# Forgetting attention: the value products of four key blocks issued together, and the PSUM buffers split anew

## The chip, the cores and the metric

The kernel runs on one core of one Trainium2 chip. The metric is the device time of one execution in microseconds (us). Engines are named as in the profile: PE (TensorE matmuls), PEld (its weight loads), DVE (VectorE), ACT (ScalarE), POOL (GpSimd), SP (SyncE, which issues the DMAs).

## The reference, cut to what matters

One layer of a decoder trunk: an RMSNorm, one input projection, three mixers (gMLP, HGRN2, forgetting attention), gates, an output projection with a residual, a final RMSNorm. The change lies in the attention: 4096 tokens, 8 heads of 64 channels, all in float32.

```python
def _fox_mixer(q, k, v, f_logit, b_f):
    ...
    log_f = jax.nn.log_sigmoid(f_logit.astype(jnp.float32) + b_f.astype(jnp.float32))
    c = jnp.cumsum(jnp.transpose(log_f, (0, 2, 1)), axis=-1)
    scale = C_HEAD_DIM ** -0.5
    ...
        s = jnp.einsum('bhqd,bhkd->bhqk', qh[:, :, q0:q1], kh[:, :, :q1]).astype(jnp.float32) * scale
        s = s + c[:, :, q0:q1, None] - c[:, :, None, :q1]
        ...
        p = jax.nn.softmax(s, axis=-1)
        outs.append(jnp.einsum('bhqk,bhkd->bhqd', p.astype(vh.dtype), vh[:, :, :q1]))
    ...
```

The result is multiplied by `silu(c_z)` and goes into the output projection.

## The kernel before, in words

Phase 1 (up to line 1069) makes the projections and the other two mixers and stores queries, keys (each as a high and a low part), values, gates and cumulative sums in DRAM. Phase 3 (from line 1391) is the output projection. Phase 2, from line 1074, is the attention.

Phase 2 works in 32 units: 4 pairs of heads `p` times 8 groups `Q` of 512 queries. A unit goes over its `4 * (Q + 1)` key blocks of 128 keys; that makes 576 steps `(u, kb)` in the loop at line 1330. The last four blocks of a unit are on the diagonal and narrower (`q0_of`). Scores stand transposed, keys on the partitions and queries in the free dimension.

One step does, for each of the two heads, a score tile: two products into a `ps_st` buffer (lines 1353, 1356), the exponential on ACT into a tile `pt` of pool `pp` (line 1360), on the diagonal a mask on POOL (line 1365). Then come row-max products, and the values of the step before (`do_pv`, line 1228): two products into `pv`, one for each head and each half of the partitions (line 1238; in the profile `128*64`, four instructions), and the sums of the weights over the keys, `acc`, head 0 on DVE and head 1 on POOL (line 1247).

The row-max pass is a generator, `rowmax` (line 1128). Each `rm_step` issues one product of 128 queries and 512 keys into one of four `ps_sm` buffers (`rm_product`, line 128) and its maximum on DVE (line 137, on the diagonal line 132). It runs ahead of the steps by `LEAD` = 76 products; a step issues two, a third one while it is behind. `rm_tail` turns a unit's maxima into rows (a transpose on PE, line 1166).

At a unit's end `finish_unit` is a generator that `tick(fin)` moves on, once per step: load the gate; `pl`, the sums over the partitions, two products in a `ps_sm` buffer (line 1206); log and exponential on ACT (lines 1210, 1211), a Newton step on DVE and POOL (lines 1213 to 1216), the product with `pv` on DVE (line 1218), the store.

PE's order is the order of the source (`manual_schedule` for PE alone); on the other engines the tile framework places instructions by its own plan. Eight PSUM buffers of 128x512 float32 are in use: two `st`, four `sm`, two `pv`. The loads of keys and values, `load_next`, have 26 slots (`slots`, ten of them with values, `vslots`) and are given back in the loop when the last unit of a head pair passes a group of keys (lines 1334 to 1339).

Of the kernel before, what the change touches and what calls it, by code (L numbers as in the profile page):

```python
# [10 lines left out]
F32 = mybir.dt.float32  # L11
# [5 lines left out]
ALU = mybir.AluOpType  # L17
# [4 lines left out]
P = 128  # L22
# [11 lines left out]
def tile_trunk(  # L34
# [42 lines left out]
    # units of attention whose row maxima are found before the last projections  # L77
# [13 lines left out]
    def rsqrt_small(pool, ssum, n, scale, tag, y=None):  # L91
        """[P, n] sums -> 1/sqrt(sum * scale + EPS), full float32 accuracy."""
# [30 lines left out]
    def rm_product(ps, qb, kb, hi_, diag, tri, dst):  # L123
        """scores of 128 queries and 512 keys of one head, and their row maxima"""
        h, i = divmod(hi_, 4)
        use = P * (i + 1) if diag else 512
        n = max(use, 256)
        nc.tensor.matmul(  # L128
            ps[:, :n], qb[0:66, h, i * P : (i + 1) * P], kb[0:66, h, :n], start=True, stop=True
        )  # L130
        if diag:
            nc.vector.tensor_tensor_reduce(
                ps[:, :use], ps[:, :use], tri[:, 512 - use :], 1.0, -3.0e38,
                op0=ALU.add, op1=ALU.max, accum_out=dst,
            )
        else:
            nc.vector.tensor_reduce(dst, ps[:, :use], axis=AX.X, op=ALU.max)  # L137

    def rm_rows(p, Q, mp, mm, m2):
        """row maxima over all key groups, less the offset: high and low parts, negated"""  # L140
# [16 lines left out]
    # =====================================================================  # L157
    # Phase 1: RMSNorm, input projection, gMLP, HGRN2, FoX operands
    # =====================================================================
    with ExitStack() as p1:  # L160
# [68 lines left out]
        def xnorm(i0, n):  # L229
            """generator: reciprocal RMS of n token tiles from i0."""  # L230
# [8 lines left out]
        def xprep(T, own_norm=False):  # L239
            """generator: hT[T] = (hi, lo), [P, KC, 256] each."""  # L240
# [43 lines left out]
        def setup_gen():  # L284
            # gMLP
# [23 lines left out]
            # keep source position s (partition) <= target position t  # L309
# [7 lines left out]
            # softmax over the single layer, cumulative sum less its first row  # L317
# [17 lines left out]
            # mixing is linear: LayerNorm's gain goes after it, and its offset  # L335
            # becomes off[t, c] = ln_b[c] * sum_s w[t, s] + b_s[t]
# [6 lines left out]
            # masks of the levels inside a block of 32: [source s, targets in second halves]  # L343
# [7 lines left out]
            for li, h in enumerate(levels[2:]):  # L351
# [4 lines left out]
                # s - 2h*n >= 0  # L356
# [4 lines left out]
                # 2h*n + h - 1 - s >= 0  # L361
# [9 lines left out]
            # head selector columns  # L371
# [5 lines left out]
            # carried state, block-diagonal over the two heads of a tile  # L377
# [4 lines left out]
            # scores: zero for good where the source is in a later block than the target  # L382
# [13 lines left out]
        def hgrn(T):  # L396
            """generator for 256 tokens (two chunks), after its inputs are on chip."""
            z, qf, v = Zb.pop(T), Qf.pop(T), Vb[T]
            lb, oml = setup["lb"], setup["oml"]
            # sigmoid(z) = exp(-L), sigmoid(-z) = exp(-(z + L)), L = ln(1 + exp(-z))  # L400
# [28 lines left out]
            for st in range(len(levels) + 4):  # L429
                if st == 1:  # L430
                    dq = sm.tile([P, 8], F32, tag="dq", name="dq")
                    nc.vector.tensor_copy(dq, pd.rearrange("p c n -> p (c n)"))
                    sc = hg_state["sc"][0]  # r, (chunk, a), t
                    hg_state["sc"].rotate(-1)
                    # blocks of 32 on the diagonal, side by side
                    s32 = wk.tile([P, 8, 32], F32, tag="s32", name="s32", bufs=1)  # (chunk, a, r), t
# [6 lines left out]
                # take over the level scores  # L443
# [24 lines left out]
                # q / k times decay to the middle of each block  # L468
                li = st
                if 0 <= li < 7:  # L470
# [14 lines left out]
                    else:  # L485
                        # both heads' targets side by side, each over zeros in the other's rows
# [12 lines left out]
                if st == 7:  # L499
                    # carry terms  # L500
# [29 lines left out]
                # level products: the two heads of a tile go to different banks  # L530
# [87 lines left out]
            # RMS norm over the value channels  # L618
# [14 lines left out]
        def cgen(B):  # L633
# [12 lines left out]
            # log1p(e) = ln(u) + (e - (u - 1)) / u  # L646
# [43 lines left out]
            # reference offsets of each 512-query group, on all partitions  # L690
# [24 lines left out]
        def silu(ps, dst, scale=1.0):  # L715
            """dst = scale * silu(ps), scale a power of two; dst holds scale * ps meanwhile."""
# [775 lines left out]
```

## Time and profile before

| | |
|---|---|
| median of 3 runs | 3517.5 us (3510.7 to 3524.14) |
| profiled execution | span 3516.6 us from the first to the last instruction; no separate time is listed for it, and the median of the runs lies 0.9 above the span |
| busy shares | PE 97%, PEld 73%, DVE 71%, ACT 45%, POOL 40% |
| mean granted PE clock | 0.982 |
| phase 2, 1674 to 3157 us | PE busy 1467, PEld 715, DVE 1248, ACT 737, POOL 895 us of 1483 |

A row of the timeline gives start and duration in us, engine, source line, operation, tiles (out<-in), shape, and how many equal instructions were merged (x4); in brackets the idle time before it and what ended it. A group of instructions shows busy us, mean ns of one, then the engine's idle time before them and who ended it. PE's durations overlap, because matmuls are pipelined; what a product takes of PE's time is the distance from its start to the next start.

### The profile page before, as it was taken

The numbers are of one execution on the slowest core, as the hardware profiler recorded it, in microseconds if no ns is written. First come the engines' busy times: TensorE is split into PE (matmuls) and PEld (weight loads), VectorE is DVE, ScalarE is ACT, GpSimd is POOL, SyncE is SP. The second block draws the span as 40 slices with busy tenths as digits, with TensorE's granted clock in tenths as the row PEclk, the third lists the DMA queues.
The fourth block names the chain that finished last, engine by engine and source line by source line (L and its number), as shares of the span: only waits on it lengthen the run. The fifth ranks groups of instructions, "written<-read, shape, count | busy, mean of one in ns | idle before, by whom it ended". The sixth has DMA issues, their size and how long they took to land.

```text
span 3516.6 us, 63564 instructions
## 1 busy us (share of the span) xinstructions
PE 3417.2 (97%) x24375; PEld 2569.8 (73%) x24375; DVE 2482.6 (71%) x5111; ACT 1584.4 (45%) x2883; POOL 1422.0 (40%) x1468
## 2 busy tenths in 40 slices
PE   7999999999999999988999999999999999999999
PEld 7999999999999998988444444444444444448887
DVE  6467746685467756782798878888889888965554
ACT  6335544356435543452345445454544554562221
POOL 2134422333134322352465466555665666570000
PEclk9999999999999999999799899999999999999999
DMA  5332333214332223212731141014101321013442
GB/s 178 109 94 64 97 127 116 79 53 159 97 104 68 70 85 111 67 49 78 155 77 34 49 118 43 19 41 120 55 28 28 97 64 37 28 64 135 148 146 96
DMA packets 227603, 297.75 MB, mean 85 GB/s; under 512 B 19602, under 2 KB 172448, under 8 KB 227298
## 3 DMA queue, kind: packets, MB, share of 16 engines
q1 hardware_dynamic: 227298, 293.69, 27.7%
q8 instruction: 191, 3.13, 0.4%
q14 instruction: 114, 0.93, 0.1%
HBM read 208.96 MB, written 84.43 MB: 83 GB/s over the span
## 4 chain that ended last, share of the span: by engine, by line
PE 76%; DVE 13%; ACT 4%; POOL 3%; issue 2%; DMA 2%; SPq 0%; DVEq 0%; POOLq 0%; ACTq 0%
PE acc L885 15%; PE pv L1238 13%; PE acc L906 12%; PE o L1430 10%; PE sm L128 9%; PE st L1353 7%; PE st L1356 6%; DVE wlo L211 2%; DVE acc L1247 1%; DMA x<-in_x_dram 1%; DVE mp L137 1%; PE pl L1206 1%; DVE gt L729 1%; DVE xq L494 1%; PE plb L557 1%
## 5 line engine op out<-in xcount | busy, mean ns | idle before, releaser
L1360 ACT ACTIVATE pt<-st,bias 128x512 f32<-128x512 f32 (+3 forms) x1152 | 692.0, 648 | 711.3 <-PE st L1356 699.3
L1247 POOL TENSOR_TENSOR acc<-acc,pt 128x512 f32<-128x512 f32 (+3 forms) x544 | 700.4, 1288 | 479.9 <-ACT pt L1360 469.4
L137 DVE TENSOR_REDUCE mp<-sm 128x1 f32<-128x512 f32 x896 | 590.1, 682 | 100.1 <-PE sm L128 92.3
L1238 PE MATMUL pv<-pt,v 128*64 128x512 f32 (+3 forms) x2304 | 587.7, 589 | 7.2 <-POOL pt L1365 4.5
L885 PE MATMUL acc<-hhi,whi 128*128 128x256 f32 x2048 | 580.7, 288 | 4.2 <-DVE q L718 2.3
L885 PE MATMUL acc<-hhi,wlo 128*128 128x256 f32 x2048 | 568.1, 282 | 0.0
L885 PE MATMUL acc<-hlo,whi 128*128 128x256 f32 x2048 | 567.3, 281 | 0.0
L906 PE MATMUL acc<-whi,hhi 128*128 128x256 f32 (+1 forms) x1792 | 518.3, 289 | 18.6 <-DVE gu L727 16.0
L1247 DVE TENSOR_TENSOR acc<-acc,pt 128x512 f32<-128x512 f32 (+3 forms) x544 | 506.5, 931 | 40.9 <-ACT pt L1360 30.4
L128 PEld LDWEIGHTS sm<-kb,qb 66*128 66x128 f32 x1152 | 218.1, 192 | 416.6 <-DVE mp L137 177.4
L906 PE MATMUL acc<-wlo,hhi 128*128 128x256 f32 (+1 forms) x1792 | 507.3, 283 | 0.0
L906 PE MATMUL acc<-whi,hlo 128*128 128x256 f32 (+1 forms) x1792 | 506.9, 283 | 0.0
L128 PE MATMUL sm<-kb,qb 66*128 66x512 f32 (+2 forms) x1152 | 494.2, 436 | 5.9 <-DVE mp L137 4.5
L1353 PE MATMUL st<-qa,ka 128*128 128x512 f32 (+2 forms) x1152 | 449.3, 392 | 12.4 <-DMA ka<-d_kl 12.4
L1356 PE MATMUL st<-qc,kb 68*128 68x512 f32 (+2 forms) x1152 | 442.3, 386 | 1.1 <-DMA qc<-d_m 1.1
L885 PEld LDWEIGHTS acc<-hhi,whi 128*128 128x128 f32 x2048 | 385.0, 190 | 7.8 <-DVE q L718 2.7
L885 PEld LDWEIGHTS acc<-hlo,whi 128*128 128x128 f32 x2048 | 384.2, 190 | 0.3 <-DVE hlo L273 0.2
L885 PEld LDWEIGHTS acc<-hhi,wlo 128*128 128x128 f32 x2048 | 384.3, 190 | 0.0
L906 PEld LDWEIGHTS acc<-whi,hhi 128*128 128x128 f32 x1792 | 341.9, 191 | 22.4 <-DVE gu L727 16.6
L906 PEld LDWEIGHTS acc<-wlo,hhi 128*128 128x128 f32 x1792 | 342.3, 191 | 0.1
L906 PEld LDWEIGHTS acc<-whi,hlo 128*128 128x128 f32 x1792 | 341.7, 191 | 0.0
L211 DVE SCALAR_TENSOR_TENSOR wlo<-wraw,gT,whi 128x256 fp32r<-128x256 f32 (+1 forms) x480 | 268.6, 600 | 58.1 <-ACT whi L210 56.8
(262 smaller groups left out, 4911.1 us busy)
## 6 DMA issues: line engine op xcount, KB each, us to landing
wraw<-in_w_in_dram SPq DMA_DIRECT2D x120, 512.0 KB
x<-in_x_dram SPq DMA_DIRECT2D x88, 512.0 KB
qa<-d_qh SPq DMA_DIRECT2D x64, 256.0 KB
out_dram<-x SPq DMA_DIRECT2D x31, 512.0 KB
kb<-d_kh SPq DMA_DIRECT2D x38, 256.0 KB
d_kh<-chi SPq DMA_DIRECT2D x32, 256.0 KB
d_kl<-clo SPq DMA_DIRECT2D x32, 256.0 KB
d_qh<-chi SPq DMA_DIRECT2D x32, 256.0 KB
```

Source lines behind the costliest of these rows:

```text
L128: nc.tensor.matmul(ps[:, :n], qb[0:66, h, i * P : (i + 1) * P], kb[0:66, h, :n], start=True, stop=True)
L137: nc.vector.tensor_reduce(dst, ps[:, :use], axis=AX.X, op=ALU.max)
L211: nc.vector.scalar_tensor_tensor(lo[:, k, :n], raw, g, hi[:, k, :n].bitcast(F32), op0=ALU.mult, op1=ALU.subtract)
L494: nc.vector.tensor_tensor(xq[rows, :, r, :].rearrange("p g (n h) -> p g n h", h=h), sl(e), sl(qf), op=ALU.mult,)
L885: nc.tensor.matmul(ps[:, a, :], ww[:, k, cs], hh[:, k, :], start=n == 0, stop=n == 3 * KC - 1)
L906: nc.tensor.matmul(o, hh[:, k, ts_], ww[:, k, :width], start=n == 0, stop=n == 3 * KC - 1)
L1238: nc.tensor.matmul(pv[64 * h : 64 * h + 64, q0:], vt[:, kb % 4, 64 * h : 64 * h + 64], pts[h][:, q0:], start=kb == 0, stop=kb == nkb - 1,)
L1247: eng.tensor_tensor(a[:, q0:], a[:, q0:], pts[h][:, q0:], op=ALU.add)
L1353: nc.tensor.matmul(st[:, qm:], ka_t[g][:, h, cs], qa_t[u % 2][:, h, qm:], start=True, stop=False)
L1356: nc.tensor.matmul(st[:, qm:], kb_t[g][0:68, h, cs], qc_t[u % 2][:, h, qm:], start=False, stop=True)
L1360: nc.scalar.activation(pt[:, q0:], st[:, q0:], AF.Exp, bias=bias_of[u][:, h, kb : kb + 1])
L1430: nc.tensor.matmul(ps, a[:, k % 4, o : o + P], b[k][:, cs], start=n == 0, stop=n == 3 * KC - 1)
```

## The change

- Values: `do_pv` is called once for four key blocks. A group of eight score tiles is collected, and its 16 products (four blocks, two heads, two instructions each) are issued behind the third score tile of the next group.
- Score tiles are issued one by one (`do_tile`), with row-max steps at fixed places between them.
- Row maxima: `rm_pair` makes two products into one buffer of 2x512 and, off the diagonal, takes both maxima in one DVE instruction. Four pairs in a group of four key blocks are eight products, as before.
- PSUM: three `st` buffers of 128x512, two `sm` buffers of 128x2x512, one `pv` buffer.
- Weight sums: head 1's on POOL right after each step; head 0's on DVE with the group's values. The first block is no longer copied; the second step adds the first two tiles. `pp` has 13 buffers in place of 7.
- Unit end: ACT copies `pv` to SBUF first, `pl` goes into the `pv` buffer, and the last product moves from DVE to POOL; there are three POOL products in place of two.
- The slots of keys and values are given back in `do_pv`.

The rest of the diff removes comments. Its core:

```diff
+    def rm_pair(ps, qb, kb, hi_, diag, tri, mp, cj):
+        for n in range(2):
+            rm_matmul(ps[:, n, :], qb, kb, hi_ + n, diag)
+        if diag:
+            for n in range(2):
+                rm_max(ps[:, n, :], hi_ + n, True, tri, mp[:, hi_ + n, cj : cj + 1])
+        else:
+            rm_max(ps, hi_, False, tri, mp[:, hi_ : hi_ + 2, cj])
...
-        pp = p2.enter_context(tc.tile_pool(name="pp", bufs=7))
+        pp = p2.enter_context(tc.tile_pool(name="pp", bufs=13))
...
-        ps_st = p2.enter_context(tc.tile_pool(name="ps_st", bufs=2, space=PSUM))
-        ps_sm = p2.enter_context(tc.tile_pool(name="ps_sm", bufs=4, space=PSUM))
-        ps_pv = p2.enter_context(tc.tile_pool(name="ps_pv", bufs=2, space=PSUM))
+        ps_st = p2.enter_context(tc.tile_pool(name="ps_st", bufs=3, space=PSUM))
+        ps_sm = p2.enter_context(tc.tile_pool(name="ps_sm", bufs=2, space=PSUM))
+        ps_pv = p2.enter_context(tc.tile_pool(name="ps_pv", bufs=1, space=PSUM))
...
-            for _ in range(3 if u == 0 else 6):
+            for _ in range(2 if u == 0 else 3):
                 yield
...
         def finish_unit(u):
             p, Q = units[u]
-            pv = pv_of.pop(u)
             acc = acc_of.pop(u)
-            zt = fs.tile([P, 512], F32, tag="zt", name="zt", bufs=2)
+            t = fs.tile([P, 512], F32, tag="rt", name="rt", bufs=3)
+            nc.scalar.copy(t, pv_of.pop(u))
+            zt = fs.tile([P, 512], F32, tag="zt", name="zt", bufs=1)
             nc.sync.dma_start(zt, d_z[Q][p * P : p * P + P, :])
             yield
-            pl = ps_sm.tile([P, 512], F32, tag="sm", name="pl")
+            pl = ps_pv.tile([P, 512], F32, tag="pv", name="pl")
...
-            nc.vector.tensor_tensor(t, pl, r, op=ALU.mult)
-            nc.vector.tensor_scalar(t, t, -1.0, 2.0, op0=ALU.mult, op1=ALU.add)
-            nc.gpsimd.tensor_tensor(r, r, t, op=ALU.mult)
-            nc.gpsimd.tensor_tensor(r, r, zt, op=ALU.mult)
+            nc.vector.tensor_tensor(n, pl, r, op=ALU.mult)
+            nc.vector.tensor_scalar(n, n, -1.0, 2.0, op0=ALU.mult, op1=ALU.add)
+            nc.gpsimd.tensor_tensor(t, t, zt, op=ALU.mult)
+            nc.gpsimd.tensor_tensor(r, r, n, op=ALU.mult)
             yield
-            nc.vector.tensor_tensor(t, pv, r, op=ALU.mult)
+            nc.gpsimd.tensor_tensor(t, t, r, op=ALU.mult)
             nc.sync.dma_start(d_yc[p][Q], t)
...
+        def do_acc(u, kb, h, pt):
...
+            eng, a = (nc.vector, nc.gpsimd)[h], acc_of[u][h]
+            if Q == 0 and kb == 0:
+                eng.tensor_copy(a, pt)
+            elif Q and kb == 1:
+                eng.tensor_tensor(a, first_pt[h], pt, op=ALU.add)
+            elif kb:
+                eng.tensor_tensor(a[:, q0:], a[:, q0:], pt[:, q0:], op=ALU.add)
...
+        def do_pv(u, j, group):
...
+            for kb, pts in group:
+                q0, _ = q0_of(u, kb)
+                for h in (1, 0):
+                    nc.tensor.matmul(
+                        pv[64 * h : 64 * h + 64, q0:], vt[:, kb % 4, 64 * h : 64 * h + 64], pts[h][:, q0:],
+                        start=kb == 0, stop=kb == nkb - 1,
+                    )
+            for kb, pts in group:
+                do_acc(u, kb, 0, pts[0])
+            if j == Q:
                 fin.append(finish_unit(u))
+                tick(fin)
+            if Q == NJ - 1:
+                slots[0] += 2
+                vslots[0] += 1
...
             for h in range(2):
...
+                pts.append(do_tile(u, kb, h))
+                n = 2 * (kb % 4) + h
+                if h == 1:
+                    do_acc(u, kb, 1, pts[1])
+                if n in (0, 1, 4, 6):
+                    rm_step()
+                if n in (3, 5, 7) and rm_count[0] < 2 * si + LEAD:
+                    rm_step()
+                if n == 2 and pend is not None:
+                    do_pv(*pend)
+                    pend = None
+                if n in (4, 5, 7):
+                    tick(fin)
+            group.append((kb, pts))
+            if kb % 4 == 3:
+                pend, group = (u, kb // 4, group), []
```

More of the change, by code (lines that the diff above doesn't have):

```diff
@@ L121, in make_tri, with rm_matmul @@
         )
-    def rm_product(ps, qb, kb, hi_, diag, tri, dst):
+    def rm_matmul(ps, qb, kb, hi_, diag):
         h, i = divmod(hi_, 4)
-        use = P * (i + 1) if diag else 512
-        n = max(use, 256)
+        n = max(P * (i + 1) if diag else 512, 256)
         nc.tensor.matmul(
@@ L130, in rm_product, with rm_max @@
         )
+    def rm_max(ps, hi_, diag, tri, dst):
         if diag:
+            use = P * (hi_ % 4 + 1)
             nc.vector.tensor_tensor_reduce(
@@ L136, in rm_product @@
         else:
-            nc.vector.tensor_reduce(dst, ps[:, :use], axis=AX.X, op=ALU.max)
+            nc.vector.tensor_reduce(dst, ps, axis=AX.X, op=ALU.max)
+    def rm_product(ps, qb, kb, hi_, diag, tri, dst):
+        rm_matmul(ps, qb, kb, hi_, diag)
+        rm_max(ps, hi_, diag, tri, dst)
+    def rm_pair(ps, qb, kb, hi_, diag, tri, mp, cj):
[6 more added lines that the diff above has]
+            rm_max(ps, hi_, False, tri, mp[:, hi_ : hi_ + 2, cj])
     def rm_rows(p, Q, mp, mm, m2):
@@ L1137, in rowmax @@
                 for cj in range(Q + 1):
-                    for hi_ in range(8):
-                        ps = ps_sm.tile([P, 512], F32, tag="sm", name="sm")
-                        rm_product(
-                            ps, qb, kb_t[p * NJ + cj], hi_, cj == Q, tri, mp[:, hi_, cj : cj + 1]
-                        )
+                    for hi_ in range(0, 8, 2):
+                        ps = ps_sm.tile([P, 2, 512], F32, tag="sm", name="sm")
+                        rm_pair(ps, qb, kb_t[p * NJ + cj], hi_, cj == Q, tri, mp, cj)
                         yield
@@ L1226, in tile_trunk @@
         fin = []
[L1228 removed]
+        first_pt = {}
+        def do_acc(u, kb, h, pt):
+            p, Q = units[u]
+            q0, _ = q0_of(u, kb)
+            if kb == 0:
+                if u not in acc_of:
+                    acc_of[u] = [ac.tile([P, 512], F32, tag=f"acc{i}", name=f"acc{i}") for i in range(2)]
+                first_pt[h] = pt
+            eng, a = (nc.vector, nc.gpsimd)[h], acc_of[u][h]
[6 more added lines that the diff above has]
+        def do_pv(u, j, group):
             p, Q = units[u]
             nkb = 4 * (Q + 1)
[L1231 to L1232 removed]
+            if j == 0:
                 pv_of[u] = ps_pv.tile([P, 512], F32, tag="pv", name="pv")
[L1234 removed]
             pv = pv_of[u]
[L1236 to L1248 removed]
+            vt = v_t[p * NJ + j]
+            for kb, pts in group:
+                q0, _ = q0_of(u, kb)
+                for h in (1, 0):
[6 more added lines that the diff above has]
+            if j == Q:
                 fin.append(finish_unit(u))
+                tick(fin)
+            if Q == NJ - 1:
+                slots[0] += 2
+                vslots[0] += 1
         wo_hi, wo_lo = [], []
@@ L1304, in rm_step @@
                 next(rm)
-                rm_count[0] += 1
+                rm_count[0] += 2
             except StopIteration:
@@ L1328, in tile_trunk, with do_tile @@
             rm_step()
-        pend = None
+        def do_tile(u, kb, h):
+            p, Q = units[u]
+            g = p * NJ + kb // 4
+            cs = slice((kb % 4) * P, (kb % 4) * P + P)
+            q0, diag = q0_of(u, kb)
+            qm = min(q0, 256)
+            st = ps_st.tile([P, 512], F32, tag="st", name="st")
+            nc.tensor.matmul(
+                st[:, qm:], ka_t[g][:, h, cs], qa_t[u % 2][:, h, qm:], start=True, stop=False
+            )
+            nc.tensor.matmul(
+                st[:, qm:], kb_t[g][0:68, h, cs], qc_t[u % 2][:, h, qm:], start=False, stop=True
+            )
+            pt = pp.tile([P, 512], F32, tag="p", name="pt")
+            nc.scalar.activation(
+                pt[:, q0:], st[:, q0:], AF.Exp, bias=bias_of[u][:, h, kb : kb + 1]
+            )
+            if diag:
+                nc.gpsimd.affine_select(
+                    pt[:, q0 : q0 + P], pt[:, q0 : q0 + P], pattern=[[1, P]], compare_op=ALU.is_ge,
+                    fill=0.0, base=0, channel_multiplier=-1,
+                )
+            return pt
+        pend, group = None, []
         for si, (u, kb) in enumerate(steps):
@@ L1332, in tile_trunk @@
             nkb = 4 * (Q + 1)
-            g = p * NJ + kb // 4
-            if Q == NJ - 1 and kb % 4 == 0 and kb > 0:
-                slots[0] += 2
-                vslots[0] += 1
-            if Q == 0 and kb == 0 and p > 0:
-                slots[0] += 2
-                vslots[0] += 1
-            while g not in ka_t:
+            while p * NJ + kb // 4 not in ka_t:
                 load_next()
```

47 lines of the change are left out of this document (1 added, 46 removed).

## The prediction

> **What bounds the kernel now.** I read the page first, then busy time by stretches, then single steps of the attention stage in the timeline. The page says that PE works 97% of the span, and its chain is mostly PE's.
>
> ```profile
> span 3516.6 us, 63564 instructions
> ...
> PE 3417.2 (97%) x24375; PEld 2569.8 (73%) x24375; DVE 2482.6 (71%) x5111; ACT 1584.4 (45%) x2883; POOL 1422.0 (40%) x1468
> ...
> L1360 ACT ACTIVATE pt<-st,bias 128x512 f32<-128x512 f32 (+3 forms) x1152 | 692.0, 648 | 711.3 <-PE st L1356 699.3
> ...
> PE acc L885 15%; PE pv L1238 13%; PE acc L906 12%; PE o L1430 10%; PE sm L128 9%; PE st L1353 7%; PE st L1356 6%; DVE wlo L211 2%; DVE acc L1247 1%; DMA x<-in_x_dram 1%; DVE mp L137 1%; PE pl L1206 1%; DVE gt L729 1%; DVE xq L494 1%; PE plb L557 1%
> ```
>
> The 1152 exponentials are two heads of 576 key blocks, so 576 steps of the loop. The answer by stretches gives the attention stage, from its first score product to its last value product (columns: stretch, its length, busy us of PE, PEld, DVE, ACT, POOL, then clock, DMA share, GB/s).
>
> ```profile
> 1674.00:3157.00 1483.00, 1467.24 (x5867) 715.47 (x5868) 1248.30 (x2159) 737.33 (x1226) 894.76 (x924) 0.98 0.23 62
> ```
>
> PE is busy all the time, but busy is not streaming. One full step, PE alone:
>
> ```profile
> 2641.71 0.40 PE L1356 MATMUL st<-qc,kb 68*128 68x512 f32 x1
> 2641.94 0.39 PE L128 MATMUL sm<-kb,qb 66*128 66x512 f32 x1
> 2642.26 1.08 PE L1238 MATMUL pv<-pt,v 128*64 128x512 f32 x4
> 2643.27 0.50 PE L128 MATMUL sm<-kb,qb 66*128 66x512 f32 x1
> 2643.61 0.40 PE L1353 MATMUL st<-qa,ka 128*128 128x512 f32 x1
> 2643.84 0.40 PE L1356 MATMUL st<-qc,kb 68*128 68x512 f32 x1
> ...
> 2644.86 0.65 PE L1238 MATMUL pv<-pt,v 128*64 128x512 f32 x2
> ```
>
> From start to start, a 128*128 product of 512 columns takes 0.23 (2641.71 to 2641.94, 2643.61 to 2643.84). Before the values it takes 0.32, after them 0.34, and the values themselves (128*64 form) 1.01. The step is 2.60 (2642.26 to 2644.86). At one place the values are followed by the row sums `pl`, which have the same 128*64 form:
>
> ```profile
> 3089.21 1.08 PE L1238 MATMUL pv<-pt,v 128*64 128x512 f32 x4
> 3090.12 1.03 PE L1206 MATMUL pl<-acc,ones_v 128*64 128x512 f32 x4
> 3091.08 0.50 PE L1353 MATMUL st<-qa,ka 128*128 128x512 f32 x1
> 3091.42 0.40 PE L1356 MATMUL st<-qc,kb 68*128 68x512 f32 x1
> ```
>
> There the values take 0.91 (entry, no exit) and the row sums 0.96 (exit, no entry). So with neither they take 0.91 + 0.96 - 1.01 = 0.86. Each change of form costs, and no other engine is behind it: at the end of the stage, with no row maxima left for DVE, the numbers are the same (1.01, then 0.34).
>
> ```profile
> 3074.19 1.08 PE L1238 MATMUL pv<-pt,v 128*64 128x512 f32 x4
> 3075.20 0.50 PE L1353 MATMUL st<-qa,ka 128*128 128x512 f32 x1
> 3075.54 0.40 PE L1356 MATMUL st<-qc,kb 68*128 68x512 f32 x1
> ...
> 3076.34 1.08 PE L1238 MATMUL pv<-pt,v 128*64 128x512 f32 x4
> ```
>
> **The change part by part.** *Values of four key blocks together.* 144 groups replace 576 steps. Of four entries, three go: 3 x (0.32 - 0.23) = 0.27. Of four exits, three go: 3 x (0.34 - 0.23) = 0.33. The values themselves: 0.91 + 2 x 0.86 + 0.96 = 3.59 in place of 4 x 1.01 = 4.04, so 0.45. Together 1.05 us a group, 10.40 to 9.35, and 144 x 1.05 = 151 us. Diagonal blocks are narrower, but I take the cost of a change of form to be the same for them. This is all on the path, since PE's queue is in order and full.
>
> *What has to hide behind the 9.35 us.* I lay out one group from its first score tile: three score tiles (0.47 each) and two row-max pairs until 2.3, the values until 6.0, five tiles and two pairs until 9.35.
>
> DVE has four pair maxima and four sums `acc` of head 0. Its rows:
>
> ```profile
> 2640.83 1.48 DVE L1247 TENSOR_TENSOR acc<-acc,pt 128x512 f32<-128x512 f32 x1
> 2642.23 1.28 DVE L137 TENSOR_REDUCE mp<-sm 128x1 f32<-128x512 f32 x2
> 2643.08 1.27 POOL L1247 TENSOR_TENSOR acc<-acc,pt 128x512 f32<-128x512 f32 x1 [1.33 <-ACT pt L1360]
> 2643.43 1.48 DVE L1247 TENSOR_TENSOR acc<-acc,pt 128x512 f32<-128x512 f32 x1
> ```
>
> ```profile
> L137 DVE TENSOR_REDUCE mp<-sm 128x1 f32<-128x512 f32 x872 | 574.5, 682 | 73.8 <-PE sm L128 66.0
> L1247 DVE TENSOR_TENSOR acc<-acc,pt 128x512 f32<-128x512 f32 x448 | 457.0, 1020 | 33.7 <-ACT pt L1360 30.4 <-POOL pt L1365 1.8
> L132 DVE CUSTOM_DVE_ANT_0 sm<-sm,tri 128x512 f32<-128x512 f32 x58 | 40.1, 691 | 4.0 <-PE sm L128 3.7
> ...
> L132 DVE CUSTOM_DVE_ANT_0 sm<-sm,tri 128x128 f32<-128x128 f32 x58 | 17.6, 303 | 4.3 <-PE sm L128 3.9
> ```
>
> Two maxima take 1.28, that is 0.60 each from start to start. A pair in one instruction is not in this trace. Above it is bounded by 1.20 (two of them), below by streaming alone: (691 - 303) / 384 = 1.01 ns an element, 1.03 for 1024. I take 0.60 + 512 x 1.01 ns = 1.12, because the trace's own slope gives it. A sum takes 0.68 when POOL is quiet (2660.03 below) and 1.48 when it starts while POOL's sum runs: DVE's ends 0.56 after POOL's (2644.91 against 2644.35), so it seems to wait for it. Four sums are thus 2.7 to 5.9. I take 2.7: they are queued behind the second pair, from about 3.4, in PE's values, when the exponentials of tiles 0 to 2 are done and POOL, which now sums head 1 as each block comes, has run out. DVE then has 4 x 1.12 + 2.7 = 7.2 of 9.35, and at the upper end 4.8 + 5.9 = 10.7, which would be the bound.
>
> ACT: eight exponentials at 0.65 are 5.2 of 9.35. Three score buffers let it run on under the values. POOL: four sums at 1.27 are 5.1. The copy of a unit's first block goes on both engines for 28 of the 32 units; all that is off the path.
>
> *Two pair buffers for four single ones.* A pair's product waits for the maximum two pairs back. In the layout the tightest is the second pair of a group (PE at 1.4), whose buffer comes free at about 0.9, so nothing waits. At a unit's end something is late. The values' bank is now one: ACT copies it out, `pl` is put into it, and the next unit's values queue behind the last reader of `pl`, 4.2 us after `pl` ended (three tiles and a pair of its own group, three tiles and two pairs of the next, 0.47 each). The chain in between, in today's rows:
>
> ```profile
> 2658.05 0.60 ACT L1210 ACTIVATE rc<-pl 128x512 f32<-128x512 f32 x1 [1.89 <-PE pl L1206]
> 2658.71 1.27 ACT L1360 ACTIVATE pt<-st,bias 128x512 f32<-128x512 f32 x2
> 2659.86 0.63 ACT L1211 ACTIVATE rc<-rc 128x512 f32<-128x512 f32 x1
> 2660.03 0.68 DVE L1247 TENSOR_TENSOR acc<-acc,pt 128x512 f32<-128x512 f32 x1
> ...
> 2661.47 0.68 DVE L1213 TENSOR_TENSOR rt<-pl,rc 128x512 f32<-128x512 f32 x1
> 2662.07 0.68 DVE L137 TENSOR_REDUCE mp<-sm 128x1 f32<-128x512 f32 x1
> ```
>
> Log, exponential and product are 0.60 + 0.63 + 0.68 = 1.9, and with two or three exponentials between them 3.2 to 3.9: just inside the 4.2. But if DVE stands at that product while the next pair waits behind it, PE gets to the pair after that about 1.5 too early. Here DVE took other work first (the maximum at 2662.07 stands between L1213 and the step that follows it in the source), so I take 0.4 of the 0 to 1.5, for 32 units: 13 us. The transposes of the row maxima share the two pair slots: 29 at 0.3 (0 to 1.0), 9 us. Without row maxima, in the last 9 or so groups, eight exponentials fall into 3.7 us of tiles, and the three buffers run out: 0.6 a group, 6 us. The last group's values now come after the loop: 2 us. SP's queue: the gate's load is issued some steps earlier relative to the unit's end and waits at most for POOL's product of the unit before; key slots come free one or two steps later, with ten of the 26 to spare. Both 0; if that cover failed, a load is a few us for PE, once per head pair.
>
> Phase 1 and the output stage run the same instructions; the output's sums have two slots in place of four, and for each of them 24 products of 0.23, 5.5 us, stand against one DVE sum: 0.
>
> *The sum*, against the profiled span of 3516.6: -151 + 13 + 9 + 6 + 2 = -121, so 3396; the median of the runs is 0.9 above that span: 3397.
>
> **The clock at a unit's end.** PE's clock was halved after a pause in this stage, and not after a shorter one:
>
> ```profile
> 1972.91 1.24 PE L128 MATMUL sm<-kb,qb 66*128 66x512 f32 x4
> 1975.62 0.38 PE L1166 MATMUL mt<-ident,m 128*16 128x128 f32 x1 [1.46 <-DVE mp L132]
> ...
> 2085.06 0.39 PE L128 MATMUL sm<-kb,qb 66*128 66x512 f32 x1
> 2086.33 1.08 PE L1238 MATMUL pv<-pt,v 128*64 128x512 f32 x4 [0.88 <-DVE rt L1218]
> ```
>
> ```profile
> 1976.00:1996.00 20.00, 20.00 (x54) 10.35 (x56) 11.12 (x28) 5.59 (x10) 5.99 (x12) 0.50 0.23 54
> ```
>
> 1.46 idle was followed by 20 us at 0.50, a loss of 10; after 0.88 idle the values had their 1.08, as in a full step. [...]
>
> **The rivals.** *Unit ends halve the clock (slower).* If DVE does stand at the product of `pl`, PE idles 1.5 once per unit, beside the 1.46 above, and each such pause costs 1.5 + 10: 32 x 11.5 = 368, less 151, plus the 17 of the other terms: 3751. It turns slower once more than (151 - 17) / 11.5 = 12 of the 32 units do it. For it: today's four slots become two pairs. Against: today the unit ends pass at less than 1 us idle, and DVE's order moves.
>
> *Unit ends wait, and the clock stays.* The same pauses at their own price alone: 3397 + 32 x 1.5 - 13 = 3432. For it: the 0.88 above. Against: the 1.46.
>
> *DVE becomes the bound.* If the four sums collide with POOL as today's mean of 1.02 has it, DVE needs 4.5 + 4.1 = 8.6, still under 9.35; it takes 1.3 a sum and more to bind. At 10.0 a group the time is 3517 - 0.4 x 144 = 3459; if every sum collides, 10.7 and 3560. For it: today most sums collide. Against: in bursts under the values POOL has little to do.
>
> *The change of form is not what costs.* If each key block's first products pay their entry anew (new weights each time), only the 0.60 around them is saved: 3517 - 86 + 30 = 3461. Against: `pl` above had new weights too.
>
> *Nothing comes of it.* PE waits for DVE at every group end and the period stays 10.4: 3517.
>
> **How the numbers follow.** Forecast 3397: 0.69, own range 3360 to 3430. Waits at unit ends with the clock left: 0.05. DVE the bound: 0.08, three quarters of it faster. Form not the cost: 0.06. Nothing: 0.04. Clock halved at unit ends: 0.08. The range 3355 to 3465 holds the forecast, the second rival and most of the two near 3460: 0.69 + 0.05 + 0.10 = 0.84. Below, all the small terms at 0 would give 3366. Faster by over 0.5% (17.6 us, about what can be told from no change here): 0.69 + 0.05 + 0.06 + 0.06 = 0.86; within it the 0.04 and part of DVE's case, 0.05; slower 0.09.
>
> **What would show it.** In the changed kernel 16 value products stand in a row and take about 3.6 us from the first to the next 128*128 product, with one 0.32 before and one 0.34 after; full groups repeat every 9.3 to 9.4; the stage lasts about 1360. The pair maximum lies at 1.1 to 1.2, DVE's sums at 0.7 each under the values. Wrong would be: sums of 1.3 and more in the bursts, PE idle over 1 us once per unit with the clock at 0.50 behind it, or inner value products that still take 1.0 a block.

## The result, and the profile after

The changed kernel takes 3483.6 us (median of four runs, 3480.4 to 3486.9) against 3514.1 for the kernel before (3507.3 to 3524.1): a ratio of 0.9916, interval 0.989 to 0.9942. It is faster by 0.8%, where the prediction said 3397 and a range of 3355 to 3465. The direction held; some 87 us of the gain are missing. The page of the changed kernel (its profiled execution took 3480.4 us):

```profile
span 3478.6 us, 62964 instructions
PE 3324.5 (96%) x24375; PEld 2627.7 (76%) x24375; DVE 2385.7 (69%) x4615; ACT 1607.1 (46%) x2915; POOL 1458.1 (42%) x1472
PE acc L902 16%; PE pv L1274 13%; PE acc L923 12%; PE o L1475 10%; PE sm L127 6%; PE st L1374 6%; PE st L1377 5%; DVE mp L140 4%; DVE acc L1261 3%; DVE wlo L228 2%; DMA x<-in_x_dram 1%; PE pl L1223 1%; DVE gt L746 1%; DVE xq L511 1%; PE xtp L284 1%
L1261 POOL TENSOR_TENSOR acc<-acc,pt 128x512 f32<-128x512 f32 (+2 forms) x516 | 672.4, 1303 | 329.8 <-ACT pt L1381 302.0
L127 PE MATMUL sm<-kb,qb 66*128 66x512 f32 (+2 forms) x1152 | 367.0, 400 | 61.1 <-DVE mp L140 36.4
```

DVE has less work than before (2385.7 for 2482.6 us), and yet its maxima and sums hold 7% of the chain, where they held 2%: PE now waits for them. The waits of PE in the attention stage between 1680 and 3000 (total, times, longest), before the change:

```profile
PE sm L128 <- DVE mp L137: 4.5, 7, 0.7
PE sm L128 <- DVE mp L132: 0.9, 1, 0.9
```

and after it:

```profile
PE sm L127 <- DVE mp L140: 36.4, 36, 2.2
PE sm L127 <- DVE mp L135: 17.3, 27, 3.0
PE mt L1181 <- DVE mp L140: 1.9, 6, 0.6
```

So PE's waits for a row-max buffer rose from 5.4 to 53.7 us. The mean granted clock also fell, from 0.982 to 0.973: over the two spans the clock took 63 us before (0.018 x 3516.6) and 94 after (0.027 x 3478.6). These 48 and 31 us are most of what is missing. Over the whole attention stage, from its first score product to its last value product, the trace shows 1483 us before: PE pauses for 16 of them and loses 28 at half clock (half of the time at 0.50), which leaves 1439. After the change it shows 1445, with 70 and 59, which leaves 1316. PE's own work thus fell by some 123 us, and pauses and clock gave most of it back. One of the places, in the timeline of the changed kernel:

```profile
2341.76 3.65 PE L1274 MATMUL pv<-pt,v 128*64 128x512 f32 x16
...
2344.07 1.47 DVE L1261 TENSOR_TENSOR acc<-acc,pt 128x512 f32<-128x512 f32 x1
2344.95 1.73 POOL L1235 TENSOR_TENSOR rt<-rt,rc 128x512 f32<-128x512 f32 x1
2345.34 0.50 PE L1374 MATMUL st<-qa,ka 128*128 128x512 f32 x1
...
2345.64 1.59 DVE L1261 TENSOR_TENSOR acc<-acc,pt 128x512 f32<-128x512 f32 x1
2345.69 0.39 PE L1377 MATMUL st<-qc,kb 68*128 68x512 f32 x1
...
2347.01 4.48 POOL L1261 TENSOR_TENSOR acc<-acc,pt 128x512 f32<-128x512 f32 x3 [0.33 <-ACT pt L1381]
2347.15 1.25 DVE L163 TENSOR_TENSOR mm<-mm,cref 128x8 f32<-128x8 f32 x1
2348.33 0.68 DVE L1261 TENSOR_TENSOR acc<-acc,pt 128x512 f32<-128x512 f32 x1
2348.93 1.24 DVE L169 TENSOR_SCALAR m<-mm 128x8 fp32r<-128x8 f32 x1
...
2350.28 1.22 DVE L140 TENSOR_REDUCE mp<-sm 128x2 f32<-128x1024 f32 x1
2351.56 1.17 PE L127 MATMUL sm<-kb,qb 66*128 66x512 f32 x2 [2.21 <-DVE mp L140]
2353.38 0.41 PE L1181 MATMUL mt<-ident,m 128*16 128x128 f32 x1
2354.42 1.22 PE L127 MATMUL sm<-kb,qb 66*128 66x512 f32 x2 [0.62 <-DVE mp L140]
```

The values are as forecast: 16 products in 3.58 (2341.76 to 2345.34), entry 0.32, exit 0.35 (3.59, 0.32, 0.34 said). Behind them the plan goes wrong. DVE's sums stand among the maxima and start while POOL is busy, so they take 1.47 and 1.59; an addition over 128x8 elements, 0.16 where it is undisturbed (row L163 below), takes 1.25, and another small one 1.24. The pair maximum starts at 2350.28, and PE stands until 2351.56. Then the transpose takes one of the two pair buffers, and the next pair waits again. The stretches around it (length, busy us of the engines, clock, DMA share, GB/s) show what the pause costs beyond itself:

```profile
2351.60:2358.50 6.90, 6.28 (x15) 3.09 (x17) 6.06 (x8) 1.37 (x2) 1.78 (x1) 0.51 0.42 92
2358.50:2365.00 6.50, 6.50 (x29) 3.85 (x26) 2.28 (x3) 2.88 (x5) 2.21 (x2) 1.00 0.13 40
```

After 2.21 idle PE ran 6.9 us at 0.51, another 3.4 lost. In this trace half clock also came without one long pause: at 2232.17, 2590.57 and 2952.38 two waits of 0.48 and 0.38 (0.49 and 0.37 at the third), less than the 0.88 that the prediction saw go by, were followed by 3.4 us at half clock (0.50).

### The profile page after: what moved, and what is told of

It is laid out like the page before. It is cut to its first block, busy times and chain, and to the rows that moved or that the text cites. A ratio compares the mean times of both kernels' runs of the same rounds, so it can differ in the third digit from the quotient of the medians.

```text
span 3478.6 us, 62964 instructions
## 1 busy us (share of the span) xinstructions
PE 3324.5 (96%) x24375; PEld 2627.7 (76%) x24375; DVE 2385.7 (69%) x4615; ACT 1607.1 (46%) x2915; POOL 1458.1 (42%) x1472
## 4 chain that ended last, share of the span: by engine, by line
PE 71%; DVE 19%; ACT 4%; issue 3%; DMA 2%; POOL 2%; SPq 0%; DVEq 0%; ACTq 0%; POOLq 0%
PE acc L902 16%; PE pv L1274 13%; PE acc L923 12%; PE o L1475 10%; PE sm L127 6%; PE st L1374 6%; PE st L1377 5%; DVE mp L140 4%; DVE acc L1261 3%; DVE wlo L228 2%; DMA x<-in_x_dram 1%; PE pl L1223 1%; DVE gt L746 1%; DVE xq L511 1%; PE xtp L284 1%
## 5 line engine op out<-in xcount | busy, mean ns | idle before, releaser
L1381 ACT ACTIVATE pt<-st,bias 128x512 f32<-128x512 f32 (+3 forms) x1152 | 698.7, 651 | 630.2 <-PE st L1377 582.3
L1261 POOL TENSOR_TENSOR acc<-acc,pt 128x512 f32<-128x512 f32 (+2 forms) x516 | 672.4, 1303 | 329.8 <-ACT pt L1381 302.0
L140 DVE TENSOR_REDUCE mp<-sm 128x2 f32<-128x1024 f32 (+1 forms) x460 | 534.8, 1192 | 223.5 <-PE sm L127 222.7
L1274 PE MATMUL pv<-pt,v 128*64 128x512 f32 (+3 forms) x2304 | 510.1, 587 | 0.0
L1261 DVE TENSOR_TENSOR acc<-acc,pt 128x512 f32<-128x512 f32 (+2 forms) x516 | 458.8, 889 | 43.1 <-POOL pt L1386 17.1
L1374 PE MATMUL st<-qa,ka 128*128 128x512 f32 (+2 forms) x1152 | 468.4, 409 | 19.6 <-DMA v<-d_v 13.2
L127 PE MATMUL sm<-kb,qb 66*128 66x512 f32 (+2 forms) x1152 | 367.0, 400 | 61.1 <-DVE mp L140 36.4
L1274 PEld LDWEIGHTS pv<-pt,v 128*64 128x64 f32 x2304 | 159.0, 143 | 297.6 <-issue 279.7
L1374 PEld LDWEIGHTS st<-qa,ka 128*128 128x128 f32 x1152 | 221.1, 192 | 191.4 <-issue 133.1
```

What stands on the lines that cost most here:

```text
L127: nc.tensor.matmul(ps[:, :n], qb[0:66, h, i * P : (i + 1) * P], kb[0:66, h, :n], start=True, stop=True)
L140: nc.vector.tensor_reduce(dst, ps, axis=AX.X, op=ALU.max)
L1261: eng.tensor_tensor(a[:, q0:], a[:, q0:], pt[:, q0:], op=ALU.add)
L1274: nc.tensor.matmul(pv[64 * h : 64 * h + 64, q0:], vt[:, kb % 4, 64 * h : 64 * h + 64], pts[h][:, q0:], start=kb == 0, stop=kb == nkb - 1,)
L1374: nc.tensor.matmul(st[:, qm:], ka_t[g][:, h, cs], qa_t[u % 2][:, h, qm:], start=True, stop=False)
L1381: nc.scalar.activation(pt[:, q0:], st[:, q0:], AF.Exp, bias=bias_of[u][:, h, kb : kb + 1])
```

## The experiments

Each was timed against the kernel before on the same chip, which took 3508 to 3515 us there. The bands in the expectations count the changed kernel as 3484 us. Waits and groups are those between 1680 and 3000 us where nothing else is said.

**Is it DVE's order?** VectorE in program order through the attention stage:

```diff
+        order = tc.manual_schedule(engines={mybir.EngineType.DVE})
+        order.__enter__()
         pend, group = None, []
...
         drain(fin)
+        order.__exit__(None, None, None)
```

> VectorE keeps the program's order in the attention stage: two pair maxima, the four sums of head 0 behind the values, then the other pairs; in the changed kernel the scheduler had put sums, row tails and finishing steps between the maxima. Theory O (the order is what makes the pair slots late, as the prediction had it laid out in program order): the 2.3 us waits for a pair slot and the waits of the transposes go, PE's waits of the stage fall from about 131 us to below 60, the stage from 1444.9 to about 1360 to 1390, and the time to 3400 to 3430 us. Rival C (VectorE is late because its sums and small operations stand still beside GpSimd's sums, in whatever order): the waits stay above 100 us and the time within 3465 to 3500 us. Rival D (VectorE has too much work in a group for two pair slots): slower waits at every group, 3480 us or more.

Measured: 3489.1 us, ratio 0.9924 (0.99 to 0.9949); no change. DVE's groups in this run (busy us, mean ns, idle before):

```profile
L1261 DVE TENSOR_TENSOR acc<-acc,pt 128x512 f32<-128x512 f32 x372 | 309.0, 831 | 26.9 <-DVE acc L1261 0.5
L1259 DVE TENSOR_TENSOR acc<-pt 128x512 f32<-128x512 f32 x27 | 35.6, 1320 | 0.0
L1230 DVE TENSOR_TENSOR rn<-pl,rc 128x512 f32<-128x512 f32 x30 | 20.7, 691 | 43.6 <-ACT rc L1228 43.4
```

The sums became quicker (831 for 952 ns; 103 of 372 still overlap an instruction of POOL, 264 of 375 in the changed kernel), but DVE now stood 43.4 us in front of the Newton step, waiting for ScalarE, with the maxima queued behind it. Theory O falls as stated: the order alone gives nothing.

**Is it the transposes' buffer?**

```diff
-            pt = ps_sm.tile([16, P], F32, tag="sm", name="mt")
+            pt = ps_st.tile([16, P], F32, tag="st", name="mt")
```

> The transposed row maxima take a score-tile buffer (three) in place of one of the two pair buffers. Theory S (the 28 waits of 1.1 us at the transposes are the price of one pair buffer in two): these 31 us go, with the half-clock stretches behind them, and the time falls by 30 to 45 us to about 3440 to 3455. Rival O or C (VectorE is late at these places, and whoever is next waits): the waits move to a score tile or to the next pair, and the time stays within 3470 to 3495.

Measured: 3449.0 us, ratio 0.9807 (0.9779 to 0.9835): 35 us better than the changed kernel, theory S. PE's waits between 1680 and 3000 are now

```profile
PE sm L127 <- DVE mp L135: 18.6, 28, 3.0
PE sm L127 <- DVE mp L140: 17.7, 17, 2.3
```

so the waits for the pair maxima (L140) halved, those for the diagonal (L135) stayed.

**Is it GpSimd's sums?**

```diff
-                nc.tensor.matmul(pl[64 * h : 64 * h + 64, :], ones_v, acc[h], start=True, stop=True)
+                nc.tensor.matmul(pl[64 * h : 64 * h + 64, :], ones_v, acc[0], start=True, stop=True)
...
-                if h == 1:
-                    do_acc(u, kb, 1, pts[1])
```

> Left out: head 1's sums on GpSimd (both halves of the divisor come from head 0's sums). Theory C (collisions with GpSimd make VectorE late): the sums of head 0 fall from a mean of 889 ns to about 650, the 128x8 operations from up to 1.25 us to about 0.1, the waits of PE in the stage from 131 us to below 50 and the time to 3385 to 3420. Theory O (the order alone): the sums are shorter but still stand ahead of the maxima; waits of 80 to 110 us are left and the time is 3440 to 3470.

Measured: 3400.4 us, ratio 0.9677 (0.9656 to 0.9698): 83 us better, theory C. DVE's full sums and PE's waits for row maxima:

```profile
L1261 DVE TENSOR_TENSOR acc<-acc,pt 128x512 f32<-128x512 f32 x405 | 309.6, 764 | 26.4 <-ACT pt L1381 13.7 <-DVE acc L1261 0.5 <-POOL pt L1386 0.3
PE sm L127 <- DVE mp L140: 22.9, 28, 2.0
PE sm L127 <- DVE mp L135: 3.6, 8, 1.1
```

The sums fell from 952 to 764 ns, not to the 650 expected: 58 of the 405 still meet other work of POOL, mostly the products of a unit's end, and take 1234; the other 347 take 686. The waits halved, and the mean clock rose from 0.973 to 0.985. The same edit in the kernel before is the control:

> The kernel before without head 1's sums on GpSimd (left out; both halves of the divisor come from head 0's sums), as a control. If the collisions of VectorE's and GpSimd's sums cost time only where two pair buffers have replaced four single ones, the kernel before gains little: its waits for a product slot are about 11 us in the stage, so 3490 to 3512 us. If they cost the kernel before as much as the changed one (about 80 us), 3420 to 3450 us, and the collisions explain nothing of the missing gain.

Measured: 3490.1 us, ratio 0.9922 (0.9895 to 0.9948), some 25 us. The kernel before pays for the collisions too, but less than a third as much.

**Is it DVE's amount of work?**

```diff
-            nc.vector.tensor_reduce(dst, ps, axis=AX.X, op=ALU.max)
+            nc.vector.tensor_reduce(dst, ps[..., :64], axis=AX.X, op=ALU.max)
```

> Left out: the pair maxima off the diagonal read only 64 of 512 columns of each product. If VectorE's time to free a pair buffer is what stops PE (theories O and C both), its waits in the stage fall below 30 us, the half clock goes with them, the stage comes to about 1310 to 1340 and the time to 3345 to 3380: that is the floor that PE's own work sets in this form. Rival E (PE waits for ScalarE's exponentials, score buffers or value loads once the pair buffers are free): 3400 us or more, with the waits at the score tiles.

Measured: 3440.6 us, ratio 0.9788 (0.9763 to 0.9813), 43 us better; the expected floor was missed by 60. DVE's groups between 1680 and 3000, first of the changed kernel:

```profile
L140 DVE TENSOR_REDUCE mp<-sm 128x2 f32<-128x1024 f32 x427 | 508.7, 1220 | 193.0 <-PE sm L127 192.4
L1261 DVE TENSOR_TENSOR acc<-acc,pt 128x512 f32<-128x512 f32 x375 | 357.0, 952 | 12.9 <-POOL pt L1386 1.5 <-DVE acc L1261 0.5
L163 DVE TENSOR_TENSOR mm<-mp,cref 128x8 f32<-128x8 f32 x3 | 0.5, 157 | 0.0
```

then of this run:

```profile
L1261 DVE TENSOR_TENSOR acc<-acc,pt 128x512 f32<-128x512 f32 x391 | 517.5, 1323 | 41.7 <-POOL pt L1386 23.0 <-ACT pt L1381 7.9
L140 DVE TENSOR_REDUCE mp<-sm 128x2 f32<-128x128 f32 x432 | 121.2, 283 | 261.4 <-PE sm L127 261.4
```

387 us of maxima were taken away, and the sums took 160 of them back (391 of them for 375): a DVE that is free sooner starts its next sum beside POOL's work. In this run 374 of the 391 sums overlap it, in the changed kernel 264 of 375. PE kept 37.7 us of waits for row maxima (22.0 and 15.7). So neither rival: it was not ScalarE, and it is not work alone but when it starts.

**Are buffer and collisions two costs?** Both single edits together:

> Two single edits together: the transposed row maxima in a score-tile buffer, and no sums on GpSimd (left out as in the run without them). If the price of the pair buffer and the price of the collisions are separate costs, the gains of 35 and 83 us add up to 3360 to 3375 us; if both are the same lateness of VectorE, the second gives nothing on top of the first: 3390 to 3405 us.

Measured: 3370.9 us, ratio 0.9593 (0.9576 to 0.9609): they add up nearly, 113 us of 35 + 83. PE's waits for row maxima are nearly gone and clean groups follow each other every 9.32 (2205.81 to 2215.13 in the timeline):

```profile
PE sm L127 <- DVE mp L135: 3.6, 8, 1.1
PE sm L127 <- DVE mp L140: 1.5, 5, 0.5
```

```profile
2205.81 3.65 PE L1274 MATMUL pv<-pt,v 128*64 128x512 f32 x16
2215.13 3.65 PE L1274 MATMUL pv<-pt,v 128*64 128x512 f32 x16
```

**What does a batch cost?** The run with both single edits, with a group's values in two batches, behind tiles three and seven (`do_pv` then takes which half; that part of the edit is not shown):

```diff
-                if n == 2 and pend is not None:
-                    do_pv(*pend)
-                    pend = None
-                if n in (4, 5, 7):
+                if n in (2, 6) and pend is not None:
+                    do_pv(*pend, n // 4)
+                    if n == 6:
+                        pend = None
+                if n in (0, 1, 7):
```

> The run with the score-tile buffer for the transposes and without GpSimd's sums (3371 us, PE almost without waits), but the values of a group in two batches of two blocks, behind tiles three and seven, in place of one batch of four (a unit's end moves with the second batch). By the prediction's term a batch costs 1.05 / 3 = 0.35 us for going over to the values' form and back, so 144 batches more cost about 50 us: 3410 to 3435 us. Rival N (the change of form isn't what cost, and the stage became shorter by the dropped waits): 3365 to 3385 us.

Measured: 3432.7 us, ratio 0.9769 (0.9743 to 0.9795), 62 us more. But the unit's end, moved along, makes PE wait:

```profile
PE pv L1275 <- DVE rn L1230: 22.4, 27, 1.4
```

Without these 22.4 it is 39 us for 144 batches, 0.27 each, where the term had 0.35: the change of form does cost, and rival N falls. A batch of full width can be read in this run's timeline directly:

```profile
2207.83 0.39 PE L1380 MATMUL st<-qc,kb 68*128 68x512 f32 x1
2208.15 1.94 PE L1275 MATMUL pv<-pt,v 128*64 128x512 f32 x8
2210.02 0.50 PE L1377 MATMUL st<-qa,ka 128*128 128x512 f32 x1
2210.36 0.40 PE L1380 MATMUL st<-qc,kb 68*128 68x512 f32 x1
```

Eight products take 1.87, with 0.32 before and 0.34 after. The second batch thus costs 2 x 1.87 - 3.58 = 0.16 inside and 0.09 + 0.11 at its ends, 0.36 in all, the price of the prediction. That the run as a whole shows 0.27 fits the narrower batches on the diagonal, which were not summed.

**Is it the pairs?** Four single buffers and two maxima in the same banks:

```diff
-        ps_sm = p2.enter_context(tc.tile_pool(name="ps_sm", bufs=2, space=PSUM))
+        ps_sm = p2.enter_context(tc.tile_pool(name="ps_sm", bufs=4, space=PSUM))
...
-                        ps = ps_sm.tile([P, 2, 512], F32, tag="sm", name="sm")
-                        rm_pair(ps, qb, kb_t[p * NJ + cj], hi_, cj == Q, tri, mp, cj)
+                        for m in (hi_, hi_ + 1):
+                            ps = ps_sm.tile([P, 512], F32, tag="sm", name="sm")
+                            rm_product(ps, qb, kb_t[p * NJ + cj], m, cj == Q, tri, mp[:, m, cj : cj + 1])
```

> The changed kernel with four single buffers for the row maxima and a maximum of 512 columns for each product, as before the change, in the same four banks; all else as changed. If two pair buffers are what makes the changed kernel sensitive to a late VectorE, the waits for a product slot fall although VectorE has more work (two maxima of about 0.69 us for one of 1.22): 3440 to 3470 us. If VectorE's lateness is what counts, however the banks are cut, the extra 0.15 us a pair (580 pairs) make it no better: 3480 to 3520 us.

Measured: 3417.7 us, ratio 0.9724 (0.9697 to 0.9752), 66 us better, and below the lower band. DVE has more to do (1127 for 1062 us between 1680 and 3000) and PE waits less:

```profile
PE sm L127 <- DVE mp L140: 10.1, 17, 1.5
PE sm L127 <- DVE mp L135: 2.5, 4, 0.8
```

A pair buffer comes free only when both products are read, a single one after its own. With GpSimd's sums left out as well:

> The changed kernel with four single buffers for the row maxima (3418 us alone) and without GpSimd's sums (left out; 3400 us alone with pair buffers). If the two are separate costs they add up (66 + 83 us): about 3335 to 3350 us. If they are one cost, a late VectorE that only a pair buffer passes on to PE, little is left for the second edit: 3370 to 3400 us, about where the pairs without GpSimd's sums and with a buffer apart for the transposes stand (3371).

Measured: 3360.9 us, ratio 0.9574 (0.955 to 0.9597), between the two bands. The medians side by side:

| us | with GpSimd's sums | without |
|---|---|---|
| kernel before | 3514 | 3490 |
| changed kernel, two pair buffers | 3484 | 3400 |
| pairs, transposes in a score-tile buffer | 3449 | 3371 |
| four single buffers | 3418 | 3361 |

Single buffers gain 66 us with the sums and 39 without; moving the transposes alone gives 29 there, so most of the 39 may be theirs. Separate costs would have given 66 + 83 = 149 us; 123 came. So they overlap by 26 (31 by the ratios, since the runs are from different chips), and the rest is separate.

The pairs alone in the kernel before:

> The kernel before with only the row maxima changed: two pair buffers in the same four banks and one maximum for a pair, values still two products for each key block. If pair buffers pass VectorE's lateness on whatever the values do, the time rises by 20 to 70 us to 3535 to 3585, with the unit's end (its divisor takes a pair buffer too) worst. If pair buffers hurt only where VectorE gets four sums at once, behind the batch of values, the time stays at 3495 to 3525 us.

Measured: 3688.4 us, ratio 1.0507 (1.048 to 1.0533). It does not answer the question. A full step still takes 2.60 (2699.88 to 2702.48), and off the diagonal PE hardly waits for a pair (L149); its new waits between 1680 and 3100 are on the diagonal:

```profile
PE sm L128 <- DVE mp L132: 76.7, 108, 3.3
PE sm L146 <- DVE mp L149: 0.3, 1, 0.3
```

That is the edit's own doing. On the diagonal its `rm_pair` issues product, maximum, product, maximum into one buffer, and the second product waits for the first maximum (0.74 at 2186.02, 1.47 at 2190.20); the changed kernel issues both products first. Half clock comes with it: over the stage it takes 110 us for 28 before (granted clock 0.93 from 1674 to 3200, against 0.98). What pair buffers cost where the values are not batched stays open, but for the 0.3 us off the diagonal.

**Versions with the whole computation.** First, transposes in a score-tile buffer, DVE in program order, and the Newton step moved behind a step of its own:

```diff
             nc.scalar.activation(r, r, AF.Exp, scale=-1.0)
+            yield
             nc.vector.tensor_tensor(n, pl, r, op=ALU.mult)
```

> The whole computation; transposed row maxima in a score-tile buffer, VectorE in the program's order, and the two Newton steps of a unit's end one step later than ScalarE's logarithm and exponential. With VectorE's order alone the time did not move: the last groups of a unit became longer by 1.5 us (11.3 for 9.8), where VectorE stood in front of the Newton step until ScalarE was done (50 us in the stage), and the other groups shorter. If that wait ate the gain, the time falls to 3400 to 3425 us; if the order has nothing to give beside the collisions, it stays at the 3440 to 3455 of the buffer alone.

Measured: 3446.9 us, ratio 0.981 (0.9792 to 0.9829), the same as the buffer alone. Then GpSimd in program order too, with its sum of a first block held back behind the second's:

```diff
-                if h == 1:
-                    do_acc(u, kb, 1, pts[1])
+                if n == 3:
+                    do = [(kb - 1, group[0][1][1]), (kb, pts[1])]
+                    for b, t in do if kb == 1 else do[::-1]:
+                        do_acc(u, b, 1, t)
+                elif n in (5, 7):
+                    do_acc(u, kb, 1, pts[1])
```

> As the run before, with GpSimd too in the program's order, and its sum of a group's first block behind the sum of the second, so that no sum of GpSimd falls beside the value products, where VectorE has its own four. If collisions are what is left, VectorE's sums come near 690 ns (from 852 in program order), and the time is 3370 to 3400 us, near the run without GpSimd's sums; if GpSimd's own lateness comes in their place (the mask of the diagonal and the unit's end behind the sums), 3410 us or more.

Measured: 3401.4 us, ratio 0.968 (0.966 to 0.9699): the best whole version, 82 us below the changed kernel. In its timeline DVE's sums lie under the values at 0.76 each, and POOL's four stand beside DVE's maxima:

```profile
2216.44 1.89 PE L1274 MATMUL pv<-pt,v 128*64 128x512 f32 x8
2216.51 2.28 DVE L1261 TENSOR_TENSOR acc<-acc,pt 128x512 f32<-128x512 f32 x3
2219.86 5.36 POOL L1261 TENSOR_TENSOR acc<-acc,pt 128x512 f32<-128x512 f32 x4 [4.14 <-ACT pt L1381]
2219.96 1.23 DVE L140 TENSOR_REDUCE mp<-sm 128x2 f32<-128x1024 f32 x1 [1.17 <-PE sm L127]
2221.36 1.23 DVE L140 TENSOR_REDUCE mp<-sm 128x2 f32<-128x1024 f32 x1 [0.17 <-PE sm L127]
2222.76 2.36 DVE L140 TENSOR_REDUCE mp<-sm 128x2 f32<-128x1024 f32 x2 [0.17 <-PE sm L127]
```

The sums' mean came down to 825 ns, not to 690: elsewhere they still meet POOL. The moved sum without DVE's order:

> The run at 3401 us without the program order on VectorE: GpSimd alone is in program order, with its sum of a group's first block moved behind the second's; transposes in a score-tile buffer, Newton steps one step later. If the collisions fall only where both engines' orders fit, the time goes back to 3430 to 3455 us; if moving GpSimd's sum is enough, it stays at 3395 to 3415.

Measured: 3419.7 us, ratio 0.9731 (0.97 to 0.9763), between the bands: 29 us below the run with the transposes' buffer alone come with GpSimd's order, its moved sum and the later Newton steps, which were not tried apart, and 18 us need DVE's order as well. With single buffers:

> The whole computation: four single buffers, the transposes among them, with VectorE and GpSimd in program order, GpSimd's sum of a first block behind the second's, and the Newton steps one step later. If the costs are separate, the single buffers give some 20 to 35 us beside the 3401 of the same order with pairs: 3365 to 3385 us. If they are one cost: 3390 to 3405. If the two maxima for a pair (0.15 us more on VectorE) are now too much beside the sums in program order: above 3405.

Measured: 3403.8 us, ratio 0.9693 (0.9666 to 0.972): nothing on top. Where DVE is in time, cutting the banks anew gains nothing in sum; the transposes share the four buffers again here, so a small gain and a small cost may cancel. Last, ScalarE in program order:

> The run at 3401 us with ScalarE as well in program order, up to the first split of the output projection's inputs. There two casts of that split stand among the last exponentials and wait for a load, and PE waits 3.7 and 3.1 us for score tiles and then runs at half clock. If these casts are the whole cause, the two waits go and the time falls by 5 to 12 us to about 3390 to 3396; if the casts are then late for the output projection, the gain is given back there: 3398 to 3405.

Measured: 3422.1 us, ratio 0.9739 (0.9713 to 0.9766), worse than both bands. The two long waits at the end went, but PE now waits for ScalarE at unit ends throughout the stage and in the last unit (`PE st L1374 <- ACT pt L1381` 11.9 us at 32 places between 1680 and 3010, for 0.9 at three in the version at 3401). At the two places that were followed, 2145.80 and 2990.51, the logarithm and exponential of a unit's end stand before the exponentials of the score tiles, at the second also a cast of the output weights. The output stage begins with 2.3 us of waiting for a cast of its inputs.

## Why the prediction was wrong

*Values of four blocks, -151: right in kind, somewhat too large.* In full groups the form costs what was read from one place before, and clean groups come every 9.32 (9.35 said). Over the stage, PE's time without pauses and half clock fell by less, from 1439 to 1316 us in the changed kernel and to 1306 in the run with both single edits; the groups on the diagonal, taken at the full price, are the likely difference, not a shown one. With GpSimd's sums out of both kernels the change gives 3490 - 3371 = 119 us with the transposes moved and 129 with single buffers; the forecast's whole sum was 121. That these meet is partly luck: the values gave less, and the 13 us for unit ends and 9 for transposes are not in those runs.

*DVE's sums at 0.68 under the values: this step failed.* It put POOL at rest there and DVE's sums in a burst in program order. Neither was so: DVE's order is the scheduler's, and POOL's sums run through the group. The sums took 952 ns on average, the prediction's own sign of being wrong (1.3 and more in the bursts) came with the 1.47 and 1.59 above, and what is worse, a late sum delays the maximum behind it. The prediction held DVE's total against the period (7.2 of 9.35, "still under 9.35" even with collisions) and missed that two pair buffers give a maximum no room to be late. That is the 83 us of the run without GpSimd's sums, less the 25 of the control: some 58 of the 87 that are missing. The rival "DVE becomes the bound" had the cause and nearly the time (3459), but not the mechanism: DVE still idles 193 us before its pair maxima, and taking three quarters of their time away gave 43 us. Two sizes were off beside this: by its own rows DVE binds from (9.35 - 4.5) / 4 = 1.2 a sum, not 1.3, and the pair maximum took 1.22, over the 1.20 that was to bound it.

*Two pair buffers: wrong.* "Nothing waits" became 53.7 us, four single buffers in the same banks are 66 us faster, and the transposes, put at 0.3 each and 9 us, are worth 35 (29 without GpSimd's sums): 1.0 to 1.2 for each of 29, at their upper end of 1.0 or past it. These 29 and the 58 above are the 87.

*Unit ends: right in that PE does not wait for the product of `pl`*; that wait is not in the changed kernel's list. The half clock, the first rival's price, came at other places, mostly behind the waits for pair buffers, and at 31 us by the mean clock; one pause of 2.21 cost 3.4 at half clock, where the prediction had 10 after 1.46.

*The end of the stage, 6 us for exponentials: right in size, wrong in cause.* PE waits 6.1 us there for score tiles, 5.5 of them in two waits that end at 3093.77 and 3113.89. At both, a cast of the output projection's inputs (L1450) stands before the exponentials on ScalarE. It waited 4.1 us, by the trace not for a load but for DVE's subtraction of the half before it (L1451), which stood behind DVE's sums. In the version at 3401 the same pair of casts does the same. The run that moved the casts away lost time elsewhere, so their price stays open.

## What to carry to other kernels

A sum of busy times per period tells whether an engine can keep up, not whether each buffer comes back in time: with two buffers, ask how late the single release may be. Before counting on a gap under other work, look whose order puts the work there, and what the engine next door does at that moment. When DVE and GpSimd both add tiles in SBUF, give them different stretches, DVE's PSUM reductions beside GpSimd's sums: in the changed kernel a full sum took 1083 ns beside POOL and 689 without it, a pair maximum 1219 and 1222.

## What the runs showed of the hardware

In the changed kernel DVE's sums of two tiles in SBUF took longer where they met POOL's work; those below that take their input, or one of two, from PSUM did not. Over 1680 to 3080, 290 of the 406 full sums overlap a POOL instruction by more than 0.1 us and take 1083 ns on average, the other 116 take 689; the pair maxima take 1219 with POOL busy (412) and 1222 without (24). The products of `pl` in PSUM with a tile in SBUF (L1230) lie beside POOL all 31 times and take 674 to 689. Small operations are hit as well: the 128x8 additions (L163) take 157 on average without POOL (19 of them) and 1119 beside it (10), up to 1255. So is an operation with one input in SBUF (L169): 169 without POOL (17), 734 beside it (12), up to 1235. Not every one is: the small reductions from SBUF (L159) take 0.16 to 0.22 beside POOL as without it.
